# 512-column token-major products, one token tile to a PSUM bank, and MLP groups of 4, 6, 6, 6 tiles

## The chip, the cores and the metric

The kernel runs on one core of a Trainium2 chip. The metric is the time of one execution on the device in microseconds (us), as the median of several runs. Everything said of durations comes from one profiled execution of the kernel before, taken by the hardware profiler.

## The reference

Two layers (DEPTH = 2) work on 512 latent tokens and 256 context tokens of width 1024, all in fp32. In each layer the modulated input goes through one combined projection into three token mixers (retention, grouped-query attention, mLSTM), which are gated, merged and projected again; then follows a gated MLP with a width-3 convolution. Context tokens are computed in the first layer in full and in the second only as far as latent tokens read them.

```python
# per layer; SEQ = 512, CTX_LEN = 256, D_MODEL = 1024, D_FF = 2816
pl = split_proj(modulate(x, mod_l[0], mod_l[1]) @ w_in[l] + b_in[l])
pc = split_proj(modulate(xc, mod_c[0], mod_c[1]) @ w_in[l] + b_in[l])
yr_c, yr_l = retention_branch(...); ya_c, ya_l = attention_branch(...); ym_c, ym_l = mlstm_branch(...)
mix_l = gated_merge(pl[-1], yr_l, ya_l, ym_l, w_br_ret[l], w_br_att[l], w_br_mlstm[l], w_out[l])
x = layer_norm(alpha * x + mod_l[2] * mix_l, ln1_g[l], ln1_b[l])
ffn_l = conv_ffn(modulate(x, mod_l[3], mod_l[4]), w_up[l], conv_w[l], conv_b[l], w_down[l])
x = layer_norm(alpha * x + mod_l[5] * ffn_l, ln2_g[l], ln2_b[l])
```

## The kernel before

Tokens lie in tiles of 128: tiles 0 to 3 are latent, 4 and 5 context. Every large product is made of three fp32r products, so that it keeps the precision of fp32: an operand is split into a high part and a low rest (`xh`, `xl`; `ah`, `al`; `zh`, `zl`; for a weight block `wh`, `wl`), and high by high, low by high and high by low are summed in PSUM. `wblock` loads a weight block of up to 128x1024 by a DMA on the SP queue, ScalarE (ACT) casts it to `wh` (L313), VectorE (DVE) subtracts to get `wl` (L314); two such pairs exist.

Two helpers issue these products, all at line 214 (`mm`):

- `fm` (feature-major) holds 128 weight columns in the array and streams tokens past them, 512 or 256 at a time. It makes most of the input projection, the 24 merge gates, the branch projections and the MLP's up-projection.
- `tm` (token-major) holds a 128-token tile of activations in the array and streams weight columns. It moves 256 columns, and two token tiles share one PSUM bank of 512 columns. It makes the v and k/q pieces that need token rows (`tm_in`), the output projection (`wout`) and the MLP's down-projection (`wdn`). One product, the mLSTM's second half of v, carries 16 gate columns as well and so moves 272 columns with one tile to a bank (`tm_vmg`).

PSUM has a pool of 3 banks for these products (`gt`) and one of 5 (`pt`) for everything else: transposes, scores, the modulation vectors.

`accumulate` (L1099 to L1104) takes a finished `wout` or `wdn` bank: DVE multiplies it by the gate row, adds it to the residual in `X`, and in the last pass gathers LayerNorm statistics (`bn_stats`). `finish` then normalises a tile on DVE, ACT and POOL, and `to_xT` transposes it on TensorE (PE; tile `ptr`) and makes the next product's `xh` (L425) and `xl` (L426).

The MLP runs in groups of hidden feature tiles, 5, 5, 6 and 6 of the 22: a group's up-projection is made pair by pair, convolved and activated on ACT and DVE into `ah` (L1439) and `al` (L1440), and then its part of the down-projection follows, k tile by k tile; a group of n reads n-2 tiles' weights first and those of the last two after. In the first group the up-projection goes over the tokens in two passes, so that it can start while the last tiles of the preceding LayerNorm are still being made.

The order of TensorE is written by a planner: `Mixer` runs one foreground generator (`layer`) and puts in a step of a background generator (mLSTM, retention, attention, LayerNorms) whenever the planned clock has passed that step's due time. When the foreground needs something that the background has not made, the remaining steps are placed one after another with nothing between. The other engines' order is set by the scheduler.

The q and k pieces of attention are computed late in the projection, after the eight readout gates of the mLSTM and retention: k and v of attention (`tm_in(6, ...)`), then q (`tm_in(4, ...)`, `tm_in(5, ...)`).

Of the kernel before, what the change touches and what calls it, by code (L numbers as in the profile page):

```python
# [19 lines left out]
DEPTH = 2  # L20
# [7 lines left out]
GROUPS = (5, 5, 6, 6)  # L28
GOFF = (0, 5, 10, 16)
# [9 lines left out]
TM_COLS = [O_VM, O_VM + 256, O_VR, O_VR + 256, O_QA, O_QA + 256, O_KA]  # L39
# [54 lines left out]
def layout(inputs):  # L94
# [10 lines left out]
    for dst, src in ((0, O_LI), (32, O_LI + 4), (64, O_LF), (96, O_LF + 4)):  # L105
# [4 lines left out]
    A["wtm"] = np.stack([w_in[:, :, c:c + 256].reshape(DEPTH, 2, 4, 128, 256).transpose(0, 1, 3, 2, 4)  # L110
                         .reshape(DEPTH, 2, 128, 1024) for c in TM_COLS], 1)
    vg = np.concatenate([w_in[:, :, TM_COLS[1]:TM_COLS[1] + 256], w_in[:, :, O_LI:O_LI + 16]], 2)
    A["wvg"] = vg.reshape(DEPTH, 8, 128, 272).transpose(0, 2, 1, 3).reshape(DEPTH, 128, 2176)
    A["btm"] = np.stack([b_in[:, c:c + 256] for c in TM_COLS], 1)
    w = np.stack([f["w_br_mlstm"], f["w_br_ret"], f["w_br_att"]], 1).reshape(DEPTH, 3, 4, 128, 4, 256)
    A["wbr"] = w.transpose(0, 1, 4, 3, 2, 5).reshape(DEPTH, 3, 4, 128, 1024)
    w = f["w_out"].reshape(DEPTH, 2, 4, 128, 4, 256)
    A["wout"] = w.transpose(0, 4, 1, 3, 2, 5).reshape(DEPTH, 4, 2, 128, 1024)
    w = f["w_up"].reshape(DEPTH, 8, 128, 2 * NF, 128)
    A["wup"] = w.transpose(0, 3, 2, 1, 4).reshape(DEPTH, 2 * NF, 128, 1024)  # L120
    w = f["w_down"].reshape(DEPTH, NF, 128, 4, 256)
# [28 lines left out]
class Mixer:  # L150
    """Emits the steps of a foreground and of queued background generators in one TensorE order."""
# [52 lines left out]
def _program(es, nc, tc, I, OUT):  # L204
# [63 lines left out]
    bst = ctile([128, 6, 24], "bst")  # L268
# [30 lines left out]
    dr_v = [dr.tile([128, 6, 128], F32, name=f"dr_v{i}") for i in range(4)]  # L299
# [32 lines left out]
    def mod_unit(l, idx, q):  # L332
# [10 lines left out]
        if u == 0:  # L343
            part = wp.tile([128, 256], F32, name="part", tag="part", bufs=2)
# [102 lines left out]
    def tm(srcs, lhs, tiles, nks, evac, hook=None, w=256):  # L447
        per = 512 // w
        banks = [tiles[i:i + per] for i in range(0, len(tiles), per)]
        gs = [None] * len(banks)  # L450
        tot = sum(nks)
        done = 0
        for src, nk in zip(srcs, nks):
            h, l = src() if callable(src) else wblock(src, nk * w)
            for bi, ts in enumerate(banks):
                if hook:
                    yield from hook(int(done > 0), ts)
                if done == 0:
# [286 lines left out]
    def retention(l, chunks, nq):  # L745
# [6 lines left out]
        for i in range(4):  # L752
            t = St("vr")
            SP.dma_start(out=t[:, :768], in_=dr_v[i].rearrange("p c e -> p (c e)"))
            vr.append(t)
# [245 lines left out]
    def brow(l, i):  # L1001
        t = wp.tile([128, 256], F32, name="brow", tag="brow", bufs=1)
        SP.dma_start(out=t, in_=I["btm"][l, i].unsqueeze(0).to_broadcast([128, 256]))
        return t
# [84 lines left out]
    def accumulate(l, X, xslot, ts, g, q, rows, first, final):  # L1089
        hf, co = divmod(q, 2)  # L1090
        i = 0
        while i < len(ts):
            n = 1
            while i + n < len(ts) and (ts[i + n] >= 4) == (ts[i] >= 4):
                n += 1
            t = ts[i]
            tmp = stg()
            t3 = tmp[:, :256 * n].rearrange("p (t c) -> p t c", c=256)
            V.tensor_tensor(t3, g[:, i:i + n], bc(rows[int(t >= 4)][hf][:, 256 * co:256 * co + 256], 1, n), op=OP.mult)  # L1099
            xs = X[:, xslot(t):xslot(t) + n, 256 * q:256 * q + 256]  # L1100
# [8 lines left out]
    def layer(l, xT, key):  # L1109
# [18 lines left out]
        def tm_in(i, evac, tiles, hook=None):  # L1128
            b = brow(l, i)
            yield from tm([I["wtm"][l, i, 0], I["wtm"][l, i, 1]], x_lhs(xh, xl), tiles, (4, 4), lambda ts, g: evac(ts, g, b), hook)  # L1130
# [8 lines left out]
        def ev_vm(i):  # L1139
            def ev(ts, g, b):  # L1140
                for hh in range(2):
                    V.tensor_tensor(vm[2 * i + hh].rearrange("p (c e) -> p c e", c=6)[:, ts[0]:ts[0] + len(ts), 0:128],
                                    g[:, :, 128 * hh:128 * hh + 128], bc(b[:, 128 * hh:128 * hh + 128], 1, len(ts)), op=OP.add)
            return ev
# [4 lines left out]
        def tm_vmg(tiles):  # L1149
            b = brow(l, 1)  # L1150
            put = ev_vm(1)

            def ev(ts, g):
                put(ts, g[:, :, 0:256], b)
                V.tensor_copy(glt[:, 128 * ts[0]:128 * ts[0] + 128].rearrange("p (a e) -> p a e", a=4)[:, :, 0:4],
                              g[:, 0, 256:272].rearrange("p (a e) -> p a e", a=4))
            cuts = (0, 816, 1632, 2176)
            yield from tm([I["wvg"][l][:, a:b] for a, b in zip(cuts, cuts[1:])], x_lhs(xh, xl), tiles, (3, 3, 2), ev, w=272)

        def ev_vr(i):  # L1160
            def ev(ts, g, b):
                t = stg()
                n = len(ts)
                t3 = t[:, :256 * n].rearrange("p (t c) -> p t c", c=256)
                V.tensor_tensor(t3, g, bc(b, 1, n), op=OP.add)
                for hh in range(2):
                    SP.dma_start(out=dr_v[2 * i + hh][:, ts[0]:ts[0] + n], in_=t3[:, :, 128 * hh:128 * hh + 128])
            return ev

        def ev_a(i):  # L1170
            def ev(ts, g, b):
                t = stg()
                n = len(ts)
                t3 = t[:, :256 * n].rearrange("p (t c) -> p t c", c=256)
                V.tensor_tensor(t3, g, bc(b, 1, n), op=OP.add)
                c0 = (0, 256, 512)[i]
                for ti in range(n):
                    SP.dma_start(out=dr_a[ts[ti]][:, c0:c0 + 256], in_=t3[:, ti])
            return ev

        def first_tiles(hf, ts):
            if not hf and ts[0] == 4:
                mod_unit(0, 1, 2)
            for t in ts:
# [333 lines left out]
```

## Time and profile before

| | |
|---|---|
| time, median of 3 runs | 2564.7 us (2563.7 to 2565.76) |
| span of the profiled execution, first to last instruction | 2558.8 us |
| median less span | 5.9 us |
| PE busy | 2467.1 us (96%), 16552 instructions |
| DVE busy | 1585.4 us (62%), 3338 instructions |
| ACT busy | 1005.9 us (39%), 1802 instructions |
| DMA moved | 329.21 MB |

The profile names an instruction by line, engine, operation and tiles, out<-in. A matmul `g<-wh,ah` holds `ah` and streams `wh`, so it is token-major; `g<-xh,wh` is feature-major. The duration of one matmul is longer than the time from its start to the next one's start, because they are pipelined; what a stream costs is read from the starts. The own time of the profiled execution is not listed apart from its span; what lies around the span is taken as the 5.9 us by which the median exceeds it.

### The profile page before, as it was taken

What the parts mean: (1) busy time and instruction counts of PE and PEld (TensorE: products, weight loads), DVE (VectorE), ACT (ScalarE), POOL (GpSimd) and SP (SyncE); (2) the same over time, 40 slices, a digit from 0 to 9 for tenths busy, and PEclk for the clock granted to TensorE, in tenths of its full rate; (3) what the DMA queues carried; (4) which work ended last, traced back from release to release, by engine and by line L of the source; (5) the groups of instructions that cost most, each with busy time, mean ns of one, the idle gap of its engine ahead of it and who ended that gap; (6) DMA issues with size and microseconds to landing.
All of it is one profiled execution on the core that took longest, in us unless ns stands there. A gap on an engine that the chain in (4) does not pass through costs nothing.

```text
span 2558.8 us, 41711 instructions
## 1 busy us (share of the span) xinstructions
PE 2467.1 (96%) x16552; PEld 2163.6 (85%) x16552; DVE 1585.4 (62%) x3338; ACT 1005.9 (39%) x1802; POOL 92.3 (4%) x111
## 2 busy tenths in 40 slices
PE   6999999999899989999999989999999998999998
PEld 4877898888788978999898978778887888988887
DVE  5555465554476885455545684756665778855557
ACT  4422321454443464232313253433245455633332
POOL 1000001000000000000000010000110000000000
PEclk9999999999999999999999999999999999999999
DMA  7343434322454662212121375243443444533232
GB/s 254 102 164 120 144 102 138 113 81 81 150 185 132 227 239 83 83 46 79 54 74 59 95 276 170 91 153 126 158 140 123 139 158 162 182 107 99 83 104 70
DMA packets 147651, 329.21 MB, mean 129 GB/s; under 512 B 15872, under 2 KB 59136, under 8 KB 147456
## 3 DMA queue, kind: packets, MB, share of 16 engines
q1 hardware_dynamic: 147456, 326.54, 38.2%
q8 instruction: 131, 2.15, 0.3%
q14 instruction: 64, 0.52, 0.1%
HBM read 283.49 MB, written 42.99 MB: 128 GB/s over the span
## 4 chain that ended last, share of the span: by engine, by line
PE 86%; DVE 6%; DMA 3%; ACT 3%; issue 1%; POOL 0%; SPq 0%; DVEq 0%; ACTq 0%; POOLq 0%
PE g L214 72%; PE psc L214 2%; PE pAV L214 2%; PE pPT L218 2%; DVE wl L314 1%; PE pNb L214 1%; PE pNf L214 1%; PE pE L214 1%; ACT wh L313 1%; PE pp L214 1%; PE pU L214 1%; PE pO L214 1%; DMA raw<-in_wtm_dram 1%; DMA raw<-in_wmod_dram 1%; DMA stg<-dr_y 1%
## 5 line engine op out<-in xcount | busy, mean ns | idle before, releaser
L214 PE MATMUL g<-xh,wh 128*128 128x512 f32 (+1 forms) x2448 | 825.6, 352 | 11.3 <-ACT xh L1295 5.0
L214 PE MATMUL g<-xl,wh 128*128 128x512 f32 (+1 forms) x2448 | 812.0, 347 | 4.8 <-DVE xl L426 3.7
L314 DVE TENSOR_TENSOR wl<-raw,wh 128x1024 fp32r<-128x1024 f32 (+3 forms) x358 | 411.9, 1151 | 355.7 <-ACT wh L313 267.3
L313 ACT CAST wh<-raw 128x1024 fp32r<-128x1024 f32 (+3 forms) x358 | 355.5, 993 | 609.3 <-PE g L214 550.9
L214 PEld LDWEIGHTS g<-xh,wh 128*128 128x128 f32 x2448 | 465.0, 190 | 82.4 <-issue 12.9
L214 PEld LDWEIGHTS g<-xl,wh 128*128 128x128 f32 x2448 | 465.7, 190 | 61.1 <-DVE xl L426 4.2
L214 PE MATMUL g<-xh,wl 128*128 128x512 f32 (+1 forms) x2448 | 510.2, 347 | 3.0 <-DVE wl L314 3.0
L214 PEld LDWEIGHTS g<-xh,wl 128*128 128x128 f32 x2448 | 401.1, 190 | 61.4 <-DVE wl L314 3.6
L214 PE MATMUL g<-wh,ah 128*128 128x256 f32 x808 | 207.2, 284 | 3.6 <-ACT ah L1439 3.6
L214 PE MATMUL g<-wh,al 128*128 128x256 f32 x808 | 206.4, 283 | 2.7 <-DVE al L1440 2.7
L214 PE MATMUL g<-wh,xh 128*128 128x256 f32 (+1 forms) x768 | 201.1, 292 | 3.0 <-ACT wh L313 2.3
L214 PE MATMUL g<-wh,xl 128*128 128x256 f32 (+1 forms) x768 | 196.8, 287 | 1.6 <-DVE xl L426 1.5
L214 PEld LDWEIGHTS g<-wh,ah 128*128 128x128 f32 x808 | 153.1, 189 | 4.9 <-ACT ah L1439 4.2
L214 PEld LDWEIGHTS g<-wh,al 128*128 128x128 f32 x808 | 153.0, 189 | 4.1 <-DVE al L1440 3.5
L214 PEld LDWEIGHTS g<-wh,xh 128*128 128x128 f32 x768 | 149.0, 194 | 7.6 <-ACT wh L313 2.7
L214 PEld LDWEIGHTS g<-wh,xl 128*128 128x128 f32 x768 | 149.0, 194 | 2.4 <-DVE xl L426 1.9
L1400 ACT ACTIVATE tc<-g,conv 128x512 f32<-128x512 f32 (+1 forms) x142 | 97.0, 683 | 136.8 <-PE g L214 134.9
L927 ACT ACTIVATE Pe<-psc,mx 128x256 f32<-128x256 f32 (+1 forms) x144 | 80.9, 566 | 168.2 <-DVE mx L922 115.9
L214 PE MATMUL g<-wl,ah 128*128 128x256 f32 x808 | 144.0, 281 | 1.3 <-DVE wl L314 1.3
L1401 DVE SCALAR_TENSOR_TENSOR tc<-g,conv,tc 128x511 f32<-128x511 f32 (+1 forms) x142 | 88.7, 625 | 84.5 <-ACT tc L1400 83.9
L398 POOL TENSOR_TENSOR rstd<-veps,mhalf 128x1 f32<-128x1 f32 (+3 forms) x68 | 71.7, 1057 | 1823.4 <-DVE veps L396 1745.9
L214 PE MATMUL g<-wl,xh 128*128 128x256 f32 (+1 forms) x768 | 127.8, 287 | 0.9 <-DVE wl L314 0.8
(279 smaller groups left out, 3199.9 us busy)
## 6 DMA issues: line engine op xcount, KB each, us to landing
raw<-in_wup_dram SPq DMA_DIRECT2D x108, 512.0 KB, 3.5
raw<-in_wmod_dram SPq DMA_DIRECT2D x96, 512.0 KB, 5.4
raw<-in_wfm_dram SPq DMA_DIRECT2D x80, 512.0 KB, 3.4
raw<-in_wtm_dram SPq DMA_DIRECT2D x32, 512.0 KB, 5.1
raw<-in_wout_dram SPq DMA_DIRECT2D x32, 512.0 KB, 3.9
raw<-in_wbr_dram SPq DMA_DIRECT2D x28, 512.0 KB, 3.8
dr_g<-stg SPq DMA_DIRECT2D x48, 256.0 KB, 2.0
raw<-in_wdn_dram SPq DMA_DIRECT2D x20, 512.0 KB, 3.5
```

What stands on the lines that cost most here:

```text
L214: nc.tensor.matmul(out, lhsT, rhs, **kw)
L218: nc.tensor.transpose(out, in_, ident)
L313: S.copy(h[:, :n], raw[:, :n])
L314: V.tensor_tensor(l[:, :n], raw[:, :n], h[:, :n].bitcast(F32), op=OP.subtract)
L398: G.tensor_tensor(r, t, mhalf[:, :n], op=OP.pow)
L927: S.activation(pe[:, a:b], prs[si][:, :b - a], AF.Exp, bias=mx[:, 3:4], scale=0.125, accum_out=sm[:, si:si + 1])
L1400: S.activation(t[:, a:b], g, AF.Identity, bias=conv[:, jj, 3:4], scale=conv[:, jj, 1:2])
L1401: V.scalar_tensor_tensor(t[:, a + 1:b], g[:, :b - a - 1], conv[:, jj, 0:1], t[:, a + 1:b], op0=OP.mult, op1=OP.add)
```

## The change

`tm` streams 512 weight columns and gives each token tile a bank of its own; a product over more than three tiles takes the further banks from the pool of 5, as tile `gx`. A weight block of 1024 columns then holds two k tiles of 512 columns instead of four of 256. The projection's columns are regrouped: v of the mLSTM, v of retention and q of attention are 512 wide, and the gate columns travel with k and v of attention (272 columns), which thereby move from the end of the token-major work to its start. The v and q products go over two groups of tiles. `accumulate` works on one tile and 512 columns. MLP groups are 4, 6, 6, 6, and down-projection weights come in blocks of two k tiles.

```diff
-GROUPS = (5, 5, 6, 6)
-GOFF = (0, 5, 10, 16)
+GROUPS = (4, 6, 6, 6)
+GOFF = (0, 4, 10, 16)
-TM_COLS = [O_VM, O_VM + 256, O_VR, O_VR + 256, O_QA, O_QA + 256, O_KA]
+TM_COLS = [O_VM, O_VR, O_QA]
...
-    def tm(srcs, lhs, tiles, nks, evac, hook=None, w=256):
-        per = 512 // w
-        banks = [tiles[i:i + per] for i in range(0, len(tiles), per)]
...
+    def tm(srcs, lhs, tiles, nks, evac, hook=None, w=512):
+        gs = [None] * len(tiles)
         tot = sum(nks)
         done = 0
-        for src, nk in zip(srcs, nks):
+        for si, (src, nk) in enumerate(zip(srcs, nks)):
             h, l = src() if callable(src) else wblock(src, nk * w)
-            for bi, ts in enumerate(banks):
...
+            for i, t in enumerate(tiles):
                 if hook:
-                    yield from hook(int(done > 0), ts)
...
+                    yield from hook(si, t)
+                if si == 0:
+                    gs[i] = gt() if i < 3 else pt("gx")
+                for k, pi in [(k, pi) for k in range(nk) for pi in (0, 1)] + [(k, 2) for k in range(nk)]:
+                    mm(gs[i][:, :w], lhs(done + k, t, pi == 1), (l if pi == 2 else h)[:, w * k:w * k + w],
+                       start=(done + k == 0 and pi == 0), stop=(done + k == tot - 1 and pi == 2))
+                yield
                 if done + nk == tot:
-                    evac(ts, gs[bi][:, :w * len(ts)].rearrange("p (t c) -> p t c", c=w))
+                    evac(t, gs[i][:, :w])
...
+    def accumulate(l, X, xslot, t, g, q, rows, first, final):
+        tmp = stg()[:, :512]
+        V.tensor_tensor(tmp, g, rows[int(t >= 4)][q], op=OP.mult)
+        xs = X[:, xslot(t), 512 * q:512 * q + 512]
+        V.scalar_tensor_tensor(xs, xs, ALPHA if first else 1.0, tmp, op0=OP.mult, op1=OP.add)
+        if final:
+            V.bn_stats(bst[:, t, 6 * q:6 * q + 6], xs)
...
+        for ts in ((4, 5, 0), (1, 2, 3)):
+            yield from tm_kg(ts)
...
-        for i in range(2):
-            yield from tm_in(2 + i, ev_vr(i), (2, 3) if l else (0, 1, 2, 3, 4, 5))
+        for ts in ((2, 3),) if l else ((4, 5, 0), (1, 2, 3)):
+            yield from tm_in(1, ev_vr, ts)
         for f in range(4):
             yield from p_gate(1, f)
         M.add(retention(l, chunks, nq), [f"m{l}"])
-        yield from tm_in(6, ev_a(2), (0, 1, 2, 3, 4, 5))
-        for i in (0, 1):
-            yield from tm_in(4 + i, ev_a(i), tuple(range(nqt)))
+        for ts in ((0, 1), (2, 3)) if l else ((4, 5, 0), (1, 2, 3)):
+            yield from tm_in(2, ev_a, ts)
...
-                for q in range(4):
-                    yield from tm([I["wout"][l, q, 0], I["wout"][l, q, 1]], z_lhs, ts, (4, 4),
+                for q in range(2):
+                    yield from tm([I["wout"][l, q, s] for s in range(4)], z_lhs, ts, (2, 2, 2, 2),
...
-                for q in range(4):
-                    n0 = gnum - 2
-                    srcs = [I["wdn"][l, q][:, go:go + n0].rearrange("p k c -> p (k c)"),
-                            I["wdn"][l, q][:, go + n0:go + gnum].rearrange("p k c -> p (k c)")]
+                for q in range(2):
+                    srcs = [I["wdn"][l, q][:, k:k + 2].rearrange("p k c -> p (k c)") for k in range(go, go + gnum, 2)]
```

In the built program the change takes TensorE from 15282 matmuls to 12618. Of the 2664 that go, 1320 belong to the down-projection (2640 of 256 columns become 1320 of 512), 288 to the output projection (576 become 288), 1008 to the input projection (2016 become 1008) and 48 to the second layer's first MLP group, one pair of tiles of which is no longer streamed in two halves. The 272-column products keep their number. Weight blocks that ACT and DVE split go from 358 to 346, DMA issues of SP from 898 to 857.

At two places the order on TensorE moves in a way that the diff does not show. The first is the end of the second layer's attention. Before, a step of attention (scores `psc`, transposes `pPT`, value products `pAV`) is followed by foreground matmuls `g`:

```order
L214 MATMUL g<-wl,xh 128x256 x4
L214 MATMUL psc<-KH,Qe 128x512
L214 MATMUL psc<-KL,Qe 128x512
L214 MATMUL psc<-KH,Qe 128x256
L214 MATMUL psc<-KL,Qe 128x256
L218 MATMUL pPT<-ident,Pe 128x128 x6
L214 MATMUL pAV<-PT,va 64x128 x12
L214 MATMUL g<-wh,xh 128x256
L214 MATMUL g<-wh,xl 128x256
```

Now, from about the same point of the attention on, step follows step:

```order
L214 MATMUL g<-wl,xh 128x512 x2
L214 MATMUL psc<-KH,Qo 128x512
L214 MATMUL psc<-KL,Qo 128x512
L214 MATMUL psc<-KH,Qo 128x256
L214 MATMUL psc<-KL,Qo 128x256
L218 MATMUL pPT<-ident,Pe 128x128 x6
L214 MATMUL psc<-KH,Qe 128x512
L214 MATMUL psc<-KL,Qe 128x512
L214 MATMUL psc<-KH,Qe 128x256
L214 MATMUL psc<-KL,Qe 128x256
L218 MATMUL pPT<-ident,Pe 128x128 x6
L214 MATMUL pAV<-PT,va 64x128 x12
```

The closing stretch in which no foreground matmul stands between attention's matmuls holds 46 of them before and 110 now. The foreground that stood there before has been used up earlier, since k and v of attention are computed before the mLSTM starts.

The second place is the first layer's first MLP group, at the last transposes of the LayerNorm (`ptr<-ident,xn`). Before, matmuls of the first pass, 256 columns wide, follow them:

```order
L214 MATMUL pp<-raw,silc 32x256 x16
L218 MATMUL ptr<-ident,xn 128x128 x8
L214 MATMUL g<-xh,wh 128x256
L214 MATMUL g<-xl,wh 128x256
L214 MATMUL g<-xh,wh 128x256
L214 MATMUL g<-xl,wh 128x256
```

Now the second pass, 512 columns wide, which reads the transposed tile itself, follows at once:

```order
L214 MATMUL pp<-raw,silc 32x256 x16
L218 MATMUL ptr<-ident,xn 128x128 x8
L214 MATMUL g<-xh,wh 128x512
L214 MATMUL g<-xl,wh 128x512
L214 MATMUL g<-xh,wh 128x512
L214 MATMUL g<-xl,wh 128x512
```

Between the last transpose and the first matmul of the second pass stood 42 matmuls before; now there is none.

## Rows read from the trace of the kernel before

**Rows 1.** The page: span, busy times, the chain that ended last by engine.

```profile
span 2558.8 us, 41711 instructions
PE 2467.1 (96%) x16552; PEld 2163.6 (85%) x16552; DVE 1585.4 (62%) x3338; ACT 1005.9 (39%) x1802; POOL 92.3 (4%) x111
PE 86%; DVE 6%; DMA 3%; ACT 3%; issue 1%; POOL 0%; SPq 0%; DVEq 0%; ACTq 0%; POOLq 0%
```

**Rows 2.** Busy time by stretch (from:to, length, PE with its instructions, ..., clock).

```profile
1140.00:1175.00 35.00, 35.00 (x297) 35.00 (x296) 18.67 (x26) 5.24 (x8) 0.00 (x0) 1.00 0.27 91
2450.00:2510.00 60.00, 60.00 (x266) 49.70 (x265) 35.27 (x43) 25.94 (x32) 0.00 (x0) 1.00 0.28 90
```

**Rows 3.** Timeline of PE (start, duration): token-major input projection.

```profile
1800.47 0.28 PE L214 MATMUL g<-wh,xl 128*128 128x256 f32 x1
1800.59 0.28 PE L214 MATMUL g<-wh,xh 128*128 128x256 f32 x1
1800.71 0.28 PE L214 MATMUL g<-wh,xl 128*128 128x256 f32 x1
```

**Rows 4.** Timeline of PE: waits for the group's last `ah` and `al`.

```profile
1437.43 0.38 PE L214 MATMUL g<-wh,ah 128*128 128x256 f32 x1 [1.16 <-ACT ah L1439]
1438.83 0.38 PE L214 MATMUL g<-wh,al 128*128 128x256 f32 x1 [1.01 <-DVE al L1440]
...
2241.07 0.39 PE L214 MATMUL g<-wh,al 128*128 128x256 f32 x1 [0.64 <-DVE al L1440]
...
2324.12 0.39 PE L214 MATMUL g<-wh,ah 128*128 128x256 f32 x1 [0.86 <-ACT ah L1439]
2325.20 0.39 PE L214 MATMUL g<-wh,al 128*128 128x256 f32 x1 [0.69 <-DVE al L1440]
...
2518.48 0.39 PE L214 MATMUL g<-wh,ah 128*128 128x256 f32 x1 [1.54 <-ACT ah L1439]
2519.20 0.39 PE L214 MATMUL g<-wh,al 128*128 128x256 f32 x1 [0.34 <-DVE al L1440]
```

**Rows 5.** Timeline of PE: last transposes and second pass, first layer's first MLP group.

```profile
944.32 1.36 PE L218 MATMUL ptr<-ident,xn 128*128 128x128 f32 x8
...
953.47 0.50 PE L214 MATMUL g<-xl,wh 128*128 128x512 f32 x1 [2.53 <-DVE xl L426]
```

**Rows 6.** Timeline of PE: the closing attention steps of the second layer.

```profile
2108.47 0.39 PE L214 MATMUL psc<-KH,Qo 128*128 128x512 f32 x1
...
2113.60 1.54 PE L218 MATMUL pPT<-ident,Pe 128*128 128x128 f32 x6 [3.61 <-ACT Pe L927]
2115.07 2.83 PE L214 MATMUL pAV<-PT,va 128*64 128x128 f32 x24
2117.83 1.51 PE L218 MATMUL pPT<-ident,Pe 128*128 128x128 f32 x6
```

**Rows 7.** Groups of instructions, ACT, shapes apart: attention's exponentials and copies.

```profile
L927 ACT ACTIVATE Pe<-psc,mx 128x512 f32<-128x512 f32 x64 | 44.0, 688 | 132.5 <-DVE mx L922 115.9 <-DVE veps L396 16.7
L944 ACT COPY PT<-pPT 128x512 f32<-128x512 f32 x64 | 37.3, 582 | 0.7 <-PE pPT L218 0.7
```

**Rows 8.** Groups of instructions, DVE, shapes apart: a bank's evacuation; a block's split.

```profile
L1099 DVE TENSOR_TENSOR stg<-g,grow 128x512 f32<-128x512 f32 x88 | 60.6, 689 | 20.2 <-PE g L214 19.9
L314 DVE TENSOR_TENSOR wl<-raw,wh 128x1024 fp32r<-128x1024 f32 x297 | 363.1, 1222 | 279.8 <-ACT wh L313 208.1 <-PE g L214 68.1 <-ACT sq L837 1.4
```

**Rows 9.** Waits over the whole span: us in total, times, longest.

```profile
PE g L214 <- DVE glt L1155: 0.8, 2, 0.4
```

**Rows 10.** Timeline of DVE: evacuation and statistics after the program's last matmuls.

```profile
2550.81 0.42 DVE L1099 TENSOR_TENSOR stg<-g,grow 128x256 f32<-128x256 f32 x1
2551.15 0.42 DVE L1104 BATCH_NORM_STATS2 bst<-z 128x6 f32<-128x256 f32 x1
2551.48 0.41 DVE L1101 SCALAR_TENSOR_TENSOR z<-z,stg 128x256 f32<-128x256 f32 x1
2551.92 0.43 DVE L1104 BATCH_NORM_STATS2 bst<-z 128x6 f32<-128x256 f32 x1
```

More of the change, by code (lines that the diff above doesn't have):

```diff
@@ L298, in _program @@
     dr_q = [dr.tile([128, 768], F32, name=f"dr_q{i}") for i in range(4)]
-    dr_v = [dr.tile([128, 6, 128], F32, name=f"dr_v{i}") for i in range(4)]
+    dr_v = dr.tile([128, 6, 512], F32, name="dr_v")
     dr_a = dr.tile([6, 128, 768], F32, name="dr_a")
@@ L343, in mod_unit @@
         if u == 0:
-            part = wp.tile([128, 256], F32, name="part", tag="part", bufs=2)
+            part = wp.tile([128, 256], F32, name="part", tag="part", bufs=1)
             S.copy(part, pp[:, :256])
@@ L1001, in brow @@
     def brow(l, i):
-        t = wp.tile([128, 256], F32, name="brow", tag="brow", bufs=1)
-        SP.dma_start(out=t, in_=I["btm"][l, i].unsqueeze(0).to_broadcast([128, 256]))
+        t = wp.tile([128, 512], F32, name="brow", tag="brow", bufs=1)
+        SP.dma_start(out=t, in_=I["btm"][l, i].unsqueeze(0).to_broadcast([128, 512]))
         return t
@@ L1129, in tm_in @@
             b = brow(l, i)
-            yield from tm([I["wtm"][l, i, 0], I["wtm"][l, i, 1]], x_lhs(xh, xl), tiles, (4, 4), lambda ts, g: evac(ts, g, b), hook)
+            yield from tm([I["wtm"][l, i, s] for s in range(4)], x_lhs(xh, xl), tiles, (2, 2, 2, 2),
+                          lambda t, g: evac(t, g, b), hook)
         xin = Xt("xin")
@@ L1137, in layer @@
             G.memset(vm[h].rearrange("p (c e) -> p c e", c=6)[:, :, 128:129], 1.0)
[L1139 to L1144, printed above, removed]
+        vm4 = xin[:, :3096].rearrange("p (h c e) -> p h c e", h=4, c=6)
@@ L1146, in layer, with ev_vm @@
+        def ev_vm(t, g, b):
+            V.tensor_tensor(vm4[:, :, t, 0:128], g.rearrange("p (h e) -> p h e", h=4),
+                            b.rearrange("p (h e) -> p h e", h=4), op=OP.add)
         glt = St("glt")
         G.memset(glt[:, :768], 0.0)
[L1149 to L1156, printed above, removed]
-            cuts = (0, 816, 1632, 2176)
-            yield from tm([I["wvg"][l][:, a:b] for a, b in zip(cuts, cuts[1:])], x_lhs(xh, xl), tiles, (3, 3, 2), ev, w=272)
@@ L1160, in ev_vr @@
[L1160 to L1179, printed above, removed]
@@ L1181, in first_tiles, with tm_kg, ev @@
-        def first_tiles(hf, ts):
-            if not hf and ts[0] == 4:
+        def tm_kg(tiles):
+            b = brow(l, 3)
+            def ev(t, g):
+                u = stg()[:, :256]
+                V.tensor_tensor(u, g[:, 0:256], b[:, 0:256], op=OP.add)
+                SP.dma_start(out=dr_a[t][:, 512:768], in_=u)
+                V.tensor_copy(glt[:, 128 * t:128 * t + 128].rearrange("p (a e) -> p a e", a=4)[:, :, 0:4],
+                              g[:, 256:272].rearrange("p (a e) -> p a e", a=4))
+            cuts = (0, 816, 1632, 2176)
+            yield from tm([I["wkg"][l][:, a:b] for a, b in zip(cuts, cuts[1:])], x_lhs(xh, xl), tiles, (3, 3, 2), ev, w=272)
@@ L1183, in first_tiles, with ev_vr, ev_a @@
+        def ev_vr(t, g, b):
+            u = stg()[:, :512]
+            V.tensor_tensor(u, g, b, op=OP.add)
+            SP.dma_start(out=dr_v[:, t], in_=u)
+        def ev_a(t, g, b):
+            u = stg()[:, :512]
+            V.tensor_tensor(u, g, b, op=OP.add)
+            SP.dma_start(out=dr_a[t][:, 0:512], in_=u)
+        def first_tiles(si, t):
+            hf = si // 2
+            if not si and t == 4:
                 mod_unit(0, 1, 2)
-            for t in ts:
-                yield f"{key}.{t}.{hf}"
@@ L1193, in first_tiles @@
                 M.done.add("mods")
[L1194 to L1195 removed]
         if l == 0:
[L1198 to L1200 removed]
+            yield from tm_in(0, ev_vm, (4, 5, 0, 1, 2, 3), first_tiles)
         else:
```

73 lines of the change are left out of this document (21 added, 52 removed).

## The prediction

> **What bounds the kernel now.** I read the page first: PE is busy 96% of the span and the chain that ended last is 86% PE [rows 1]. So a change counts by what it does to PE's stream: how long the stream is, and where it stops. DVE at 62% and ACT at 39% matter only where PE waits for them. The profiled execution is taken as 2558.8 us of span plus the 5.9 us by which the median exceeds it, so the sum below starts at 2564.7, the median itself. A difference under 0.2% (5.1 us) can hardly be told from no change.
>
> Second, the pitch of the stream. A busy PE says nothing here, because matmuls overlap; what counts is matmuls per time. In a stretch of pure token-major down-projection 297 matmuls touch 35 us; two of them lie over its edges, so 35/295 = 118.6 ns for 256 columns. In a pure feature-major stretch 266 touch 60 us, 60/264 = 227.3 ns for 512 columns [rows 2]. In the token-major input projection starts lie 120 ns apart [rows 3]. Two matmuls of 256 columns thus take 237 to 240 ns, one of 512 takes 227: each matmul has a part that doesn't grow with its columns.
>
> Third, where PE stops next to the code that changes. At the end of an MLP group it waits for the last `ah` and `al` [rows 4]; after the first layer's LayerNorm, for `xl` [rows 5]; at the end of attention, for ACT [rows 6].
>
> **The change, part by part.**
>
> *Pitch.* The 1320 + 288 matmuls that go from down- and output projection are worth 2 x 118.6 - 227.3 = 9.9 ns each, together 15.9 us; the 1008 + 48 that go from the input projection and the first MLP group 2 x 120 - 227.3 = 12.7 ns each, 13.4 us. Sum -29.3 us, all of it on PE's stream. No row of before shows a 512-column matmul with a token tile held in the array; its pitch is bounded by 227.3 below and by 237 (two of 256, no gain at all) above, and I take 227.3, since the array sees the same shape and type. The Trainium skill, TensorE: Matmul & The Clock Gate, section Back-to-back issue gap, gives N/2.4 + 2.5 ns for an isolated matmul, which leaves a fixed 2.5 ns: 2664 matmuls would then be worth 6.7 us and the sum below would be 2574. The rows disagree with that figure (9.9 to 12.7 ns), so the sum goes by the rows.
>
> *The waits for the last feature tile.* Seven waits: 1.16 + 1.01 + 0.64 + 0.86 + 0.69 + 1.54 + 0.34 = 6.2 us [rows 4]. They arise because a product streams the first four k tiles of a 256-column piece (24 matmuls for two token tiles, 2.8 us) and then needs the group's last tile. Now the same four k tiles hold twice the columns: 24 x 227 ns = 5.4 us in the shortest case, more than the old cover and the waits after it together (2.8 + 1.54 + 0.34 = 4.7). So -6.2 us (bounds -6.2 and -4).
>
> *Weight splits and evacuation.* A split costs DVE 1.22 us [rows 8]; a block feeds at least 2 tiles x 6 matmuls x 227 ns = 2.7 us of PE, so it stays covered by the stream that it feeds, and there are 12 fewer. Were that cover gone, each block would cost PE up to 1.2 us. Evacuation of a bank keeps 0.69 us [rows 8]. The brow loads and the stores to DRAM get fewer and larger (SP issues 41 DMAs less); 12 more loads of `wtm` and 4 fewer of `wup` go to the same queue, ahead of their use by the five raw buffers. All this I cost at nothing.
>
> *k and v of attention moved ahead.* Their matmuls keep their number, but now stand before the mLSTM starts, and are missing as foreground later. At the end of the second layer 110 attention matmuls run with nothing between instead of 46: 64 more, four steps. There ACT sets the pace: per step an exponential of 0.69 us and a copy of 0.58 us for 512 keys [rows 7], with about two thirds of that again for the other 256 keys, near 2.2 us, while PE's own part is about as long. So a step may cost next to nothing (lower bound 1 us for four) or the 3.61 us wait seen once in the old bunch [rows 6] (upper bound 14 us). I take 1.5 us a step: +6. The first layer's attention ends with 24 instead of 4 in a row, and at the layer boundary the last token tiles have some 1.6 us less cover: +4 for both (0 to 6).
>
> *Groups of 4, 6, 6, 6.* The first MLP group's first pass is one pair shorter. In the first layer 42 matmuls, at the 120 ns of 256 columns [rows 3] 5.0 us, stood between the last transposes and the second pass, and still PE waited 2.53 us for `xl` [rows 5]. That cover is gone. DVE has less to do meanwhile (a pair's convolution and splits), so I give back 4 of the 5: +4 (0 to 5). In the second layer about 60 matmuls of cover remain, 7 us, and no wait is expected. What the old fifth pair did is done in later groups; the columns stay the same.
>
> *Banks.* A product over three tiles now takes all three `gt` banks, where two tiles to a bank left one free. The next product's first matmul then waits for a bank whose evacuation has only the time of two tiles, 2 x 6 x 227 ns = 2.7 us. Before, the 272-column product already had one tile to a bank, 12 banks in all, and waited 0.8 us after them [rows 9], 0.07 us a bank. Some 60 further banks are handed on in this way: +4 (0 to 9). At the start, the six transposed tiles of the first input share the pool of 5 with three `gx` that hold banks: +1.5 (0 to 3).
>
> *Given back at once.* Where PE waits for LayerNorm anyway (around the two output projections and the layer boundary), a faster stream only waits longer: +2 (0 to 3). At the very end the evacuation and statistics behind the last matmul are 512 wide: multiply, add and statistics of about 0.42 us each [rows 10] become 0.69 [rows 8], +0.8.
>
> Sum: -29.3 - 6.2 + 6 + 4 + 4 + 4 + 1.5 + 2 + 0.8 = -13.2. Predicted time 2564.7 - 13.2 = 2551.5 us.
>
> **The rivals.**
>
> *Little is given back.* With the new waits near their lower bounds (1 + 0 + 0 + 0 + 0 + 0 + 0.8) the sum is -33.7, so 2531; with half of the forecast's 22.3 it is 2540. The case lies between, at 2535. For it: DVE and ACT get less work in the stretches with waits. Against: each named cover is gone in the order of instructions. Chance 0.16.
>
> *Most is given back.* With attention's steps at 3.61 us [rows 6] (14), 5 for `xl`, 6, 4 + 1.5, 2 and 0.8, new waits are 33.3: -2.2, so 2562.5, no measurable change. For it: the old bunch did wait, and its steps run while LayerNorm's work comes to the same engines. Against: that wait was one in a bunch of three steps. Chance 0.12.
>
> *Banks decide, slower.* All 146 token-major banks are now handed from tile to tile, and DVE works in order: if work that itself waits stands ahead of an evacuation, PE stops at each hand-over. At the longest wait seen, 0.4 us [rows 9], that is 146 x 0.4 = 58 us: 2564.7 - 29.3 - 6.2 + 18.3 + 58 = 2606. It decides from 17.2/146 = 0.12 us a bank on. For it: DVE carries the evacuations of the whole kernel. Against: 12 such banks have cost 0.8 us, and products over more than three tiles have up to six banks. Chance 0.06.
>
> *The fixed part belongs to feature-major products alone.* Then 512 columns with a token tile held take 237 ns, the pitch gain is 0, and the sum is 2564.7 - 6.2 + 22.3 = 2581, slower. For it: no row of before shows the shape. Against: both kinds hold 128x128 and stream fp32r. Chance 0.04. The Trainium skill's 2.5 ns a matmul (same page and section) would end on this side too, at the 2574 above; the pitches of before don't bear it out.
>
> **How the numbers follow.** The forecast has 0.62, the rivals 0.16, 0.12, 0.06 and 0.04. Faster by over 0.2% means below 2559.6: forecast and first rival, 0.78. Within 0.2%: 0.12. Slower: 0.10. The range takes in the forecast with its bounds, the upper two thirds of the first rival and the second one: 2534 to 2564; outside lie the two slower rivals and a rest of the first, 0.17.
>
> **What would show it.** In the changed profile, groups `g` and `gx` of 128x512 with 227 ns from start to start; no wait for L1439 or L1440 at the MLP groups' ends; a wait of 5 to 7 us for `xl` before the second pass in the first layer; 110 attention matmuls in a bunch with waits for ACT or DVE of some 12 us in all; and PE's total of waits for evacuations under 5 us. A pitch above 232 ns, waits of over 14 us in the bunch, or waits for evacuations of over 17 us would make the prediction wrong.

## The result and the profile after

The changed kernel takes 2589.3 us (median of 4 runs, 2585.6 to 2592.2) against 2564.2 us: a ratio of 1.0098, 95% interval 1.0084 to 1.0112. It is slower by 25 us, where 13 us of gain were predicted. Below, every other kernel is given as its ratio to the kernel before on the same chip and, for addition, as that ratio times 2564.7 us; so the change stands at +25.1 us.

The page of the changed kernel, beside [rows 1]: span and busy times.

```profile
span 2586.8 us, 36205 instructions
PE 2464.4 (95%) x13888; PEld 2031.8 (79%) x13888; DVE 1580.9 (61%) x3226; ACT 1011.0 (39%) x1782; POOL 90.6 (4%) x111
```

PE is as busy as before with 2664 fewer matmuls: busy time says nothing here. So the stream is taken apart as in the prediction, into pitch and stops. For each matmul the time to the next one's start is taken; its usual pitch is the mean, for its kind, of those within 30 ns of the median; what is above is a stop. A stop so counted is either a wait or a stretch in which matmuls come more slowly than usual. Worked out from all matmul records, in us:

| stops of PE | before | after | by pairs | three undone | + qdr on POOL |
|---|---|---|---|---|---|
| head, to the first feature-major product | 33.8 | 46.3 | 33.6 | 32.9 | 32.7 |
| layer 1, projection to attention | 58.3 | 65.8 | 66.1 | 65.7 | 54.9 |
| output projection, first MLP group | 22.6 | 37.6 | 31.5 | 29.1 | 29.6 |
| rest of the MLP | 8.0 | 3.2 | 3.2 | 3.4 | 3.5 |
| layer boundary | 29.5 | 25.6 | 27.5 | 24.5 | 25.7 |
| layer 2, projection to attention | 37.1 | 46.3 | 44.2 | 46.8 | 41.8 |
| output projection, first MLP group | 25.2 | 36.7 | 35.8 | 29.8 | 27.3 |
| rest of the MLP | 4.6 | 1.9 | 1.9 | 1.8 | 1.8 |
| all stops | 219.1 | 263.5 | 243.7 | 233.9 | 217.1 |
| all pitches | 2325.9 | 2309.2 | 2306.8 | 2311.6 | 2314.2 |

(The last three columns are experiments below.) The pitches fell by 16.7 us, the stops rose by 44.4. By the same records some 30 of the 44 us are time in which PE stood idle; the rest is matmuls that come more slowly: the granted clock averages 0.983 over the span, 0.989 before. The prediction had no term for that. Each column is one execution, and executions of one kernel differ by some us. Where PE waited most, in the view of waits:

```profile
PE pp L214 <- DMA raw<-in_wmod_dram: 17.8, 14, 3.9
PE ptr L218 <- ACT xn L1078: 16.8, 6, 5.9
PE g L214 <- ACT xh L425: 10.7, 5, 3.2
PE g L214 <- DVE wl L314: 8.7, 6, 3.8
PE g L214 <- DVE xl L426: 7.2, 5, 2.6
PE psc L214 <- ACT Pe L923: 6.6, 5, 3.9
...
PE pU L214 <- DVE kd L515: 3.6, 1, 3.6
...
PE g L214 <- DVE glt L1142: 0.9, 2, 0.6
...
PE g L214 <- ACT ah L1410: 0.5, 1, 0.5
```

The waits for the last `ah` and `al` [rows 4] are down to 0.5 us. Banks handed on late are no matter: `glt` has 0.9 us [rows 9]. The first line, loads of the modulation weights, was 16.6 us before and is no news. Grown are `xh` at L425 (2.5 us before), `psc` (0.5), `ptr` (12.8), `wl` (5.1), `xl` (5.2) and `kd` (2.3 in two waits, the longest 1.6).

**The pitch.** Busy time by stretch, changed kernel, beside [rows 2]: down-projection, then token-major input projection, both 512 columns.

```profile
1165.00:1195.00 30.00, 30.00 (x131) 24.31 (x130) 12.92 (x17) 4.50 (x5) 0.00 (x0) 1.00 0.17 53
1575.00:1595.00 20.00, 20.00 (x90) 16.57 (x89) 4.06 (x4) 2.99 (x3) 0.00 (x0) 1.00 0.16 43
```

Counted as before: 30/129 = 232.6 ns with `ah` held, 20/88 = 227.3 ns with `xh` held. (One matmul more or less in such a stretch moves the figure by some 2 ns. Over all matmul records, within 30 ns of the median, it is 232.0 ns with `ah` held and 226.6 to 228.7 with `xh` held.)

**The head.** Timeline of PE, changed kernel: six tiles of the first input.

```profile
30.53 0.80 PE L214 MATMUL g<-wh,xh 128*128 128x512 f32 x1 [2.11 <-ACT xh L425]
...
33.55 0.75 PE L218 MATMUL ptr<-ident,xt 128*128 128x128 f32 x4
34.23 1.07 PE L214 MATMUL pp<-raw,silc 128*32 128x256 f32 x16
36.54 0.51 PE L214 MATMUL g<-wh,xh 128*128 128x512 f32 x1 [1.24 <-ACT xh L425]
...
39.22 0.60 PE L218 MATMUL ptr<-ident,xt 128*128 128x128 f32 x4
42.15 0.50 PE L214 MATMUL g<-wh,xh 128*128 128x512 f32 x1 [2.33 <-ACT xh L425]
```

PE transposes a tile (`ptr`) and needs the same tile's `xh` next. ACT and DVE have to turn it round in between, and PE stands. The granted clock falls as well, to 0.83 from 1.00 (third figure from the end); the same stretch of the changed kernel, then of the kernel before:

```profile
40.00:60.00 20.00, 13.14 (x67) 7.86 (x67) 7.12 (x18) 6.96 (x14) 2.40 (x4) 0.83 0.36 117
```

```profile
40.00:60.00 20.00, 17.71 (x154) 16.53 (x154) 15.73 (x41) 13.76 (x29) 4.05 (x6) 1.00 0.36 121
```

**A weight split that comes late.** DVE and then PE of the changed kernel, layer 1, q product of attention:

```profile
396.05 1.92 DVE L765 TENSOR_TENSOR qdr<-qr,qt 64x768 f32<-64x768 f32 x2
398.00 1.23 DVE L314 TENSOR_TENSOR wl<-raw,wh 128x1024 fp32r<-128x1024 f32 x1
```

```profile
399.29 1.22 PE L214 MATMUL g<-wl,xh 128*128 128x512 f32 x2 [3.84 <-DVE wl L314]
400.30 0.63 PE L214 MATMUL g<-wh,xh 128*128 128x512 f32 x1
400.73 0.63 PE L214 MATMUL g<-wh,xl 128*128 128x512 f32 x1
```

```profile
400.00:403.00 3.00, 3.00 (x11) 2.33 (x10) 2.97 (x8) 0.00 (x0) 0.00 (x0) 0.59 0.61 191
403.00:410.00 7.00, 7.00 (x42) 6.05 (x41) 5.96 (x15) 2.97 (x7) 0.00 (x0) 1.00 0.40 113
```

Since 388.4 DVE has scaled retention's queries (`qdr`, eight operations of about 0.96 us) and states; the split of the next block stands behind them. Behind the stop, matmuls come 0.43 us apart, not 0.227: the lower of the two clock levels. By 403 us the granted clock is back at 1.00. (The Trainium skill, TensorE: Matmul & The Clock Gate, section Back-to-back issue gap, gives N/1.2 ns at the lower level, 427 ns for 512 columns; the trace agrees.) So this stop costs its 3.84 us and, for the eight matmuls from 399.29 to 402.70, 3.41 - 8 x 0.227 = 1.6 us more.

**The second pass without its cover.** PE of the changed kernel, first layer's first MLP group, beside [rows 5]:

```profile
973.55 0.80 PE L214 MATMUL g<-xh,wh 128*128 128x512 f32 x1 [3.16 <-ACT xh L425]
976.92 0.80 PE L214 MATMUL g<-xl,wh 128*128 128x512 f32 x1 [2.58 <-DVE xl L426]
```

Together 5.7 us, where it was 2.53: the 5 to 7 us that the prediction named as a sign.

### The profile page after: what moved, and what is told of

It reads as the page before. It is cut to its first block, busy times and chain, and to the rows that moved or that the text cites. A ratio compares the mean times of both kernels' runs of the same rounds, so it can differ in the third digit from the quotient of the medians.

```text
span 2586.8 us, 36205 instructions
## 1 busy us (share of the span) xinstructions
PE 2464.4 (95%) x13888; PEld 2031.8 (79%) x13888; DVE 1580.9 (61%) x3226; ACT 1011.0 (39%) x1782; POOL 90.6 (4%) x111
## 5 line engine op out<-in xcount | busy, mean ns | idle before, releaser
L314 DVE TENSOR_TENSOR wl<-raw,wh 128x1024 fp32r<-128x1024 f32 (+2 forms) x346 | 418.8, 1211 | 391.1 <-ACT wh L313 312.4
L313 ACT CAST wh<-raw 128x1024 fp32r<-128x1024 f32 (+2 forms) x346 | 360.4, 1042 | 637.4 <-PE g L214 354.4
L214 PE MATMUL g<-wh,xh 128*128 128x512 f32 (+1 forms) x384 | 143.8, 380 | 8.6 <-ACT xh L425 5.7
L1371 ACT ACTIVATE tc<-g,conv 128x512 f32<-128x512 f32 (+1 forms) x140 | 96.2, 687 | 137.6 <-PE g L214 135.7
L214 PE MATMUL g<-wh,xl 128*128 128x512 f32 (+1 forms) x384 | 140.2, 371 | 1.7 <-DVE xl L426 1.7
L1372 DVE SCALAR_TENSOR_TENSOR tc<-g,conv,tc 128x511 f32<-128x511 f32 (+1 forms) x140 | 88.3, 631 | 86.1 <-ACT tc L1371 86.0
L214 PE MATMUL g<-wl,xh 128*128 128x512 f32 (+1 forms) x384 | 109.6, 372 | 5.4 <-DVE wl L314 5.3
L214 PE MATMUL g<-wh,ah 128*128 128x512 f32 x280 | 111.5, 398 | 1.0 <-DVE tc L1379 0.8
L214 PE MATMUL g<-wh,al 128*128 128x512 f32 x280 | 110.4, 394 | 0.0
L214 PEld LDWEIGHTS g<-wh,xh 128*128 128x128 f32 x384 | 73.3, 191 | 24.2 <-ACT xh L425 6.8
L1373 DVE SCALAR_TENSOR_TENSOR tc<-g,conv,tc 128x511 f32<-128x511 f32 (+1 forms) x140 | 88.8, 635 | 4.4
L214 PE MATMUL g<-wl,ah 128*128 128x512 f32 x280 | 87.7, 394 | 0.0
```

What stands on the lines that cost most here:

```text
L214: nc.tensor.matmul(out, lhsT, rhs, **kw)
L313: S.copy(h[:, :n], raw[:, :n])
L314: V.tensor_tensor(l[:, :n], raw[:, :n], h[:, :n].bitcast(F32), op=OP.subtract)
L1371: S.activation(t[:, a:b], g, AF.Identity, bias=conv[:, jj, 3:4], scale=conv[:, jj, 1:2])
L1372: V.scalar_tensor_tensor(t[:, a + 1:b], g[:, :b - a - 1], conv[:, jj, 0:1], t[:, a + 1:b], op0=OP.mult, op1=OP.add)
L1373: V.scalar_tensor_tensor(t[:, a:b - 1], g[:, 1:b - a], conv[:, jj, 2:3], t[:, a:b - 1], op0=OP.mult, op1=OP.add)
```

## The experiments

**Groups of 5, 5, 6, 6 again** in the changed kernel.

```diff
-GROUPS = (4, 6, 6, 6)
+GROUPS = (5, 5, 6, 6)
```

(A group of 5 then has one block of a single k tile.)

> The changed kernel (2589 us) with MLP groups of 5, 5, 6, 6 again. Groups theory: the shorter first pass took PE's cover for the LayerNorm tiles; the stops in the stretch from the output projection to the first group (38 us in the first layer, 37 in the second, against 23 and 26 before) go back by some 10 us in the first layer and 5 in the second, so 2572 to 2580 us. Rival, the 512-wide products themselves make the stops (later hand-over of X rows and weights): 2586 to 2592 us, stops unchanged within 4 us.

Measured: 2592.4 us, ratio 1.0103 (1.0088 to 1.0118), +26.4 us. No gain, though with intervals of this size one of 4 us could hide. In its trace the stops from the output projection to the first group are some 7 us fewer in layer 1, about the expected 10, and no fewer in layer 2. The reverse, groups of 4, 6, 6, 6 in the kernel before:

> The kernel before with MLP groups of 4, 6, 6, 6 and nothing else. The prediction priced the shorter first pass at 4 us (and undoing it in the changed kernel moved nothing, 2592 us against 2589): 2566 to 2570 us by the prediction's term, 2562 to 2566 us if later groups' ends or stops give it back.

Measured: 2566.9 us, ratio 1.0006 (0.9997 to 1.0015), +1.5 us. In its trace the stops at layer 1's first group grow as the prediction's term has it (21.2 against 16.2 us), but the time can't be told from no change. The groups aren't the cause of the 25 us.

**The first tiles by pairs** in the changed kernel.

```diff
-            yield f"{key}.{t}.{hf}"
+            if t in (4, 0, 2):
+                for u in (t, t + 1):
+                    yield f"{key}.{u}.{hf}"
```

(The modulation products that the same hook places, `pp`, go back to their old places with it.)

> The changed kernel with the first input's transposes asked for by pairs of tiles, as before, instead of tile by tile. Head theory: PE transposes a tile and needs it at once; one tile ahead, the stops of the first 112 us fall from 46 to about 34 us, so 2575 to 2580 us. Rival, the six banks held at once (three of them from the pool of 5) starve the transposes: the stops stay above 42 us, 2586 to 2592 us.

Measured: 2568.0 us, ratio 1.0016 (1.0007 to 1.0025), +4.1 us: 21 us of the 25 are gone. Timeline of PE of this kernel, the same tiles:

```profile
34.99 0.92 PE L218 MATMUL ptr<-ident,xt 128*128 128x128 f32 x4
35.67 0.47 PE L214 MATMUL g<-wh,xh 128*128 128x512 f32 x1
...
37.13 0.60 PE L218 MATMUL ptr<-ident,xt 128*128 128x128 f32 x4
37.66 1.07 PE L214 MATMUL pp<-raw,silc 128*32 128x256 f32 x16
39.13 0.50 PE L214 MATMUL g<-wh,xh 128*128 128x512 f32 x1 [0.40 <-ACT xh L425]
```

The tile used after a transpose is the one transposed before it; a wait of 2.11 or 2.33 us becomes 0 to 0.4. The head's stops are back at 33.6 us, so the six banks held at once, the rival, cost nothing here. The head ends 15.4 us earlier (first feature-major product at 96.2, not 111.6 us): 12.7 of stops; the rest is that its transposes `ptr` usually come 109 ns apart, in the changed kernel's head 211. The other 6 us lie at layer 1's first group (31.5 against 37.6 us of stops) and in layer 2, where no code differs; why, and whether each execution shows it, is left open.

**k and v of attention late again** in the changed kernel.

```diff
-    kg = np.concatenate([w_in[:, :, O_KA:O_KA + 256], w_in[:, :, O_LI:O_LI + 16]], 2)
+    kg = np.concatenate([w_in[:, :, O_VM + 256:O_VM + 512], w_in[:, :, O_LI:O_LI + 16]], 2)
...
+        yield from tm_half(1, 3, 0, put_ka, (0, 1, 2, 3, 4, 5))
         for ts in ((0, 1), (2, 3)) if l else ((4, 5, 0), (1, 2, 3)):
             yield from tm_in(2, ev_a, ts)
```

> The changed kernel with k and v of attention made late again (256 columns a matmul, 96 more matmuls, about 1 us of pitch; the gate columns travel with half of the mLSTM's v, as before). Filler theory: attention's steps get their foreground matmuls back; the stops in attention and the closing bunch fall by 10 to 15 us over both layers, 2573 to 2580 us. Rival, the bunch's steps are set by ACT whatever stands between and the stops come from the 512-wide q and v products' weight blocks: no gain, 2587 to 2593 us.

Measured: 2580.2 us, ratio 1.0060 (1.0047 to 1.0074): 9.7 us gained. This edit does two things: besides moving k and v it makes half of the mLSTM's v 256 wide again and sends the other half along with the gates. By the pages it has 288 matmuls more than the changed kernel (14176 against 13888), not 96; at the prediction's 12.7 ns each they cost 3.7 us, so without them it would have gained some 13 us.

The closing bunch of layer 2, beside [rows 6], has its longest wait with and without the filler; the changed kernel, then this one:

```profile
2130.71 0.58 PE L214 MATMUL psc<-KH,Qe 128*128 128x256 f32 x1 [3.87 <-ACT Pe L923]
```

```profile
2133.50 0.89 PE L220 MATMUL pPT<-ident,Pe 128*128 128x128 f32 x6 [4.03 <-ACT Pe L925]
```

What goes are shorter waits: in all PE waits 7.8 us in the bunch of the changed kernel, 5.3 here and 3.6 in the kernel before. The stops from layer 2's output projection to the first group fall from 36.7 to 30.1 us. That fits the filler theory; that the rest of the 9.7 us comes from filler, and not from the other half of the edit, isn't shown.

**All three undone:** the three diffs above together.

> All three undone at once: what is left is the 512-wide products with a bank to a tile. If order and groups made all the new stops, the stops are back at 219 us less the 6 us for the last ah and al, and the shorter stream (17 us) shows: 2540 to 2548 us, faster than before. If the 512-wide products make stops of their own, 2555 to 2575 us. If neither, 2585 to 2592 us.

Measured: 2557.5 us, ratio 0.9975 (0.9966 to 0.9985), -6.4 us. Faster than before, yet in the middle case: the stops are 14.8 us above those of before, 7.4 in layer 1 and 9.7 in layer 2 between projection and attention. Some of that is this one execution: it took 2562.7 us, 5.2 above its kernel's median, while that of the kernel before, a span of 2558.8 plus the 1.7 to 2.3 us that lie around the span in the other runs, was some 3.5 below the median.

**Retention's scaled queries on POOL,** with all three undone.

```diff
-                V.tensor_tensor(q[64 * d:64 * d + 64, :nq].rearrange("p (c t) -> p c t", c=nch),
+                G.tensor_tensor(q[64 * d:64 * d + 64, :nq].rearrange("p (c t) -> p c t", c=nch),
```

> The kernel with all three undone (2557.5 us), and retention's scaled queries (qdr, sixteen DVE operations of 0.7 to 1 us) on POOL. Theory: the two longest new stops, 3.87 us and 2.92 us for wl in the q product of either layer, arise because these stand ahead of the weight split in DVE's order; they go, and with them the low clock after each: 8 to 11 us, 2547 to 2550 us. Rival: retention then waits for POOL, or the split is late for other reasons; 2555 to 2560 us.

Measured: 2546.2 us, ratio 0.9933 (0.9921 to 0.9946), -17.2 us; 10.8 us from this line. Waits for `wl` in the kernel with all three undone, and in this one:

```profile
PE g L216 <- DVE wl L316: 10.5, 5, 3.9
```

```profile
PE g L216 <- DVE wl L316: 3.7, 3, 3.0
```

Whether the change made these stops is seen by the same edit in the kernel before:

> The kernel before with retention's scaled queries (qdr) on POOL and nothing else. If the stops for wl behind qdr are new with the products by trips, there is little to gain here (it waited 1.6 us for kd there): 2561 to 2565 us. If qdr on POOL is worth 11 us by itself: 2553 to 2555 us.

Measured: 2562.5 us, ratio 0.9993 (0.9982 to 1.0004). Nothing clear of noise is gained there. An explanation, worked out and not tested by itself: a block of q then fed six tiles of 256 columns, 72 x 120 ns = 8.6 us; by trips it feeds three tiles of 512, 18 x 227 ns = 4.1 us, less than DVE's row of `qdr`. And in the changed kernel alone:

> The changed kernel (2589.3 us) with retention's scaled queries (qdr) on POOL and nothing else. It has one stop of 3.84 us for wl in the first layer's q product and one of 3.64 us for kd in the second layer's retention. If both stand behind qdr on DVE they go, and with the low clock behind each the kernel gains 8 to 11 us as the kernel with all three undone did: 2578 to 2582 us. If that gain needs the old places of the k and v product: 2586 to 2591 us.

Measured: 2583.4 us, ratio 1.0072 (1.0057 to 1.0088): 6.7 us gained, under the expected range. The stop at 399 us is gone. In layer 2 the wait for `kd` is gone, but another has come:

```profile
1795.01 1.22 PE L214 MATMUL g<-wl,xh 128*128 128x512 f32 x2 [4.63 <-DVE wl L314]
```

DVE and POOL just ahead of it:

```profile
1784.49 13.82 POOL L765 TENSOR_TENSOR qdr<-qr,qt 64x512 f32<-64x512 f32 x8 [6.50 <-ACT qt L730]
```

```profile
1787.62 1.78 DVE L737 TENSOR_TENSOR rmask<-rmask,df 128x512 f32<-128x512 f32 x1
...
1792.68 4.49 DVE L314 TENSOR_TENSOR wl<-raw,wh 128x1024 fp32r<-128x1024 f32 x2
```

With k and v made early, q's blocks meet the start of retention, and beside POOL these DVE operations take about twice as long (below).

**Output and down-projection alone** in the kernel before: `wout`, `wdn` and `accumulate` as changed, all else as before.

```diff
-                for q in range(4):
-                    yield from tm([I["wout"][l, q, 0], I["wout"][l, q, 1]], z_lhs, ts, (4, 4),
+                for q in range(2):
+                    yield from tm([I["wout"][l, q, s] for s in range(4)], z_lhs, ts, (2, 2, 2, 2),
...
-                for q in range(4):
-                    n0 = gnum - 2
+                for q in range(2):
+                    ks = [(k, min(k + 2, go + gnum)) for k in range(go, go + gnum, 2)]
```

> The kernel before with only the output and down-projection 512 columns wide, a bank to a tile (1608 of the 2664 matmuls saved); order, groups and input projection as before. Theory, the 512-wide form itself is cheap and the q and v products by trips (a weight block now feeds half as much PE time) made the rest of the stops: 1608 x 4.8 ns = 7.7 us of pitch and some 6 us of waits for the last ah and al are gained, little is lost, 2549 to 2554 us, clearly better than the 2557.5 us with all three undone. Rival, the wider evacuations at a product's end hold up LayerNorm: the stops from the output projection to the first group grow by 6 us or more in each layer, 2557 to 2563 us.

Measured: 2556.6 us, ratio 0.9966 (0.9953 to 0.9979), -8.7 us. Between the cases: the stops at the first groups are 28.6 and 30.0 us against 22.6 and 25.2. In layer 1, DVE's last statistics of the output projection, and PE's last matmuls of it, in the kernel before and in this one:

```profile
901.41 0.63 PE L214 MATMUL g<-wl,zh 128*128 128x256 f32 x4
...
904.21 0.42 DVE L1104 BATCH_NORM_STATS2 bst<-xres 128x6 f32<-128x256 f32 x1
```

```profile
900.61 0.62 PE L214 MATMUL g<-wl,zh 128*128 128x512 f32 x2
...
907.86 0.68 DVE L1096 BATCH_NORM_STATS2 bst<-xres 128x6 f32<-128x512 f32 x1
```

The statistics end 2.6 us after the last matmul before, 7.3 us after it now: the last pass over three tiles now evacuates half rows of all of them, where it was quarter rows.

**The down-projection alone** in the kernel before: the second half of the diff above without the first.

> The kernel before with only the down-projection 512 columns wide; the output projection stays 256 wide with two tiles to a bank. With both wide (2556.6 us) the stops from the output projection to the first MLP group were 28.6 us in the first layer and 30.0 in the second, against 22.6 and 25.2 before. Evacuation theory: six half-tile evacuations come at the end of a product over three tiles, LayerNorm's statistics come 5 us later after the last matmul; undone, these stops are back within 2 us, 288 matmuls lose 1.4 us: 2547 to 2551 us. Rival, the stops come from elsewhere (the matmul order, chance): 2555 to 2560 us.

Measured: 2551.0 us, ratio 0.9937 (0.9924 to 0.9950), -16.2 us. Of the 6.0 and 4.8 us that both wide products add to the stops at the first groups, its trace has 2.5 us fewer in layer 1 and 4.5 in layer 2: back within 2 us in layer 2 alone.

**The output projection 256 wide,** in the kernel with all three undone and `qdr` on POOL.

```diff
-                for q in range(2):
-                    yield from tm([I["wout"][l, q, s] for s in range(4)], z_lhs, ts, (2, 2, 2, 2),
+                for q in range(4):
+                    yield from tm4([I["wout"][l, q, 0], I["wout"][l, q, 1]], z_lhs, ts, (4, 4),
```

> The fastest so far (2546.2 us: all three undone and qdr on POOL), with the output projection 256 wide and two tiles to a bank, as before. By the evacuation theory 8 to 10 us of stops between output projection and first MLP group go and 1.4 us of pitch comes back: 2538 to 2541 us. By the rival 2546 to 2549 us.

Measured: 2546.3 us, ratio 0.9921 (0.9908 to 0.9933), -20.3 us. The stops move as the evacuation theory has it (first groups 23.9 and 24.5 us, 8.5 less), but the time moves by 3 us with overlapping intervals. Between the two kernels above it was 7.5 us (-8.7 and -16.2). So the wide output projection costs something from 0 to 8 us, which isn't settled. This kernel and the one with `qdr` on POOL are the fastest found, 17 to 20 us under the kernel before.

**Held tiles placed otherwise,** in the kernel with output and down-projection alone.

```diff
-        return sp.tile([128, 774], dt, name=name, tag="S", bufs=16)
+        return sp.tile([128, 784], dt, name=name, tag="S", bufs=16)[:, :774]
```

> The same with the tiles that hold ah, al, zh and zl 784 instead of 774 columns apart (3136 instead of 3096 bytes a row), and one part buffer instead of two to make room. Down-projection's matmuls come every 232 ns, where the input projection's (xh held) come every 227 to 228. If the placing of the held tiles does that, the pitch falls to 227 to 228 ns, worth 1608 x 4.5 ns = 7 us; if not, 232 ns stays and the time is that of the kernel with 774 within 3 us.

Measured: 2552.8 us, ratio 0.9957 (0.9943 to 0.9971), within the other's interval. Down-projection in it:

```profile
1145.00:1175.00 30.00, 30.00 (x131) 24.41 (x130) 11.90 (x17) 3.35 (x4) 0.00 (x0) 1.00 0.22 70
```

30/129 = 232.6 ns, as with 774. The placing isn't it.

## Why the prediction was wrong, point by point

The prediction gave "slower" a chance of 0.10, and for other causes. From its -13.2 to the measured +25.1 us are 38.3 us: the head's hook has 19.5 of them (21.0 by its experiment, less the 1.5 that were counted), the pitch 8.5, the late `qdr` 6.7; 3.6 are left for all other terms.

- *Pitch, -29.3.* The 13.4 us of `xh` held at 227.3 ns is confirmed. The 15.9 us of down- and output projection rested on "I take 227.3, since the array sees the same shape and type". It is 232.6: 1608 x (2 x 118.6 - 232.6) = 7.4 us. The term is -20.8, inside its bounds, 8.5 us too good, at a pitch at the edge of the 232 ns that the prediction named as a sign of being wrong. (The table has -16.7, since the head's transposes count there at the 211 ns of their slow stretch; in the kernel by pairs it is -19.1.) The fixed part of 2.5 ns that the Trainium skill states (TensorE: Matmul & The Clock Gate, section Back-to-back issue gap) is nearer the 2 x 118.6 - 232.6 = 4.6 ns of these products than the 12.7 ns of the input projection.
- *Waits for the last feature tile, -6.2.* Right: 0.5 us are left of them.
- *Head, +1.5.* **The step that failed.** It reads "the six transposed tiles of the first input share the pool of 5 with three `gx` that hold banks", and looked at banks alone. The change turns `for t in ts: yield` in the first product's hook into one tile a step, so that PE asks for a tile at the moment it needs it: the term had the banks, which cost nothing, and left out the wait for the turn-round. Undoing that was worth 21 us, 15 of them seen in the head.
- *Weight splits, nothing.* **The second failure:** "a block feeds at least 2 tiles x 6 matmuls x 227 ns = 2.7 us of PE, so it stays covered by the stream that it feeds". The cover was weighed against the split's own 1.22 us, not against what stands ahead of it in DVE's order, some 10 us of `qdr` and states. A stop of 3.84 us for a split, and one of 3.64 us in layer 2 for retention's `kd`, which also stood behind `qdr`, each with a spell at the lower clock behind it: 6.7 us in the changed kernel, 10.8 once k and v were late.
- *k and v of attention, +6 and +4.* The sum fits: 9.7 us, or 13 without the cost of 288 more matmuls. The parts fit less: the closing bunch waits 4.2 us more than before (7.8 against 3.6), 12 in all were expected, and at the layer boundary the stops fell from 29.5 to 25.6 us where a cost was expected. That the total agrees is in part luck.
- *Groups, +4.* The mechanism is there (5.7 us of waits before the second pass against 2.53, 5 us of stops in layer 1 in the kernel before), its time too small to tell.
- *Banks, +4.* Not at hand-overs (0.9 us). The wider evacuation costs elsewhere, in LayerNorm behind the output projection, 0 to 8 us, which no term had.

The account by the runs: undoing groups, pairs and filler one at a time gave -1.3, 21.0 and 9.7 us, 29.4 together; undoing all at once gave 31.5. What stays then, 2328 matmuls fewer (16552 less the 14224 of that kernel's page), 720 of them in the input projection, is -720 x 12.7 ns = -9.1 and -7.4 of pitch, -6.2 for `ah` and `al`, +10.8 for the late splits, +4 for LayerNorm (the middle of its range), and the +2 and +0.8 of the prediction, -5.1 us in all; measured were -6.4. So close an agreement is luck: the 10.8 and the 4 are each uncertain by about 4 us. None of the rivals was it. "Banks decide" had the right sign, for a cause that isn't there; "the fixed part belongs to feature-major products alone" was half right for one kind of product and worth 8.5 us, not 29.

## What to carry to other kernels

When a loop that prefetches by its own granularity is rewritten, look first at what runs one step ahead because of it: a hook that asked for two tiles hid a 2 us turn-round, one that asks for one hides nothing. The cover of an operation is to be weighed against the longest run of other work that can stand ahead of it in its engine's order, not against its own duration; halving what a weight block feeds made PE wait for a burst that had been there before. And wide products should first be tried one kind at a time: the down-projection alone was worth 16 us, the whole change lost 25.

## What the runs showed of the hardware that wasn't expected

- A 512-column fp32r matmul comes every 227.3 ns with `xh` held and every 232.6 ns with `ah` held, the latter with DVE or ACT at work during the matmul or not (232.0 and 231.9 ns on average over the matmul records of the changed kernel), and with either distance of the held tiles. The cause is open.
- DVE slows down beside POOL. While POOL made `qdr`, DVE's split of 1.22 us took 2.86 us in the kernel with all three undone and `qdr` on POOL, and `rmask` (0.68 us in the changed kernel) 1.63 to 1.78 us in the changed kernel with `qdr` on POOL; an operation that reads PSUM kept its 0.53 us. Both engines there, in order:

```profile
324.60 6.95 POOL L767 TENSOR_TENSOR qdr<-qr,qt 64x768 f32<-64x768 f32 x3
326.99 2.86 DVE L316 TENSOR_TENSOR wl<-raw,wh 128x1024 fp32r<-128x1024 f32 x1
329.77 0.53 DVE L1233 TENSOR_SCALAR stg<-g,bfm,gnh 128x256 f32<-128x256 f32 x1
```

The Trainium skill, GPSIMD Engine Reference, section 1. Specifications, says that POOL shares its SBUF interfaces with VectorE and that DVE instructions with two SBUF inputs contend there; the trace agrees, 1.22 against 2.86 us. Moving `qdr` to POOL was still worth 10.8 us: it ran there from 315.7 us on instead of 357.1, ahead of the q product and out of DVE's order.
